# Branch weights prepared early and kept in DRAM, Fourier parts and share loads moved, projections reordered

## The chip, the cores and the metric

The kernel runs on one core of one Trainium2 chip. The metric is the device time of one execution in microseconds (us), taken as the median of several runs. The core has five engines: TensorE (PE, matmuls; its weight loads are listed as PEld), VectorE (DVE), ScalarE (ACT), GpSimd (POOL) and SyncE (SP). In this kernel SP issues most loads, and POOL issues stores, broadcasts, gathers and accumulating transfers. Each of the two works through its transfers in the order of the program and waits in front of one whose data or buffer is not ready.

## The reference

One encoder layer on a sequence of 1024 positions with 1024 channels, in float32. The middle step, in which the change lies, is the mixer:

```python
h = x @ w_in + b_in                       # -> q, k, v (12 heads of 128), u (4 groups of 128), gates
for g, (window, dilation) in enumerate(((128, 1), (512, 4), (2048, 16))):
    o, l = dilated_window_attention(q[:, :, sl], k[:, :, sl], v[:, :, sl], rel_bias[:, sl], window, dilation)
    outs.append(o); lses.append(l)
w_mix = softmax(stack(lses), axis=0)      # shares of the three groups
attn = sum(w_mix[..., None] * stack(outs), axis=0)
four = real(fft2(u, axes=(positions, channels of the group), norm='ortho'))
merged = g_attn * (attn @ w_proj_attn) + g_four * (four @ w_proj_fourier)
return merged @ w_out
```

Before the mixer and after it stands a SwiGLU feed-forward network; each of the three steps ends in a residual sum and a layer normalization.

## The kernel before

**Numbers.** A float32 product is made of three matmuls. `split` writes a page of 128x1024 as a high part (ScalarE, a copy rounded to fp32r) and a low part (VectorE, the difference), and high x high, high x low and low x high are summed. Most products are paired in a scheme with seven half-size products instead of eight (`pair_jobs`, line 443); one such product is 12 matmuls of 128x128 by 128x512.

**Order.** Nothing runs in the order of the source. The class `Flow` (lines 72 to 257) is a planner that runs while the program is written out. PE's jobs have a fixed order. Every other step is a node with an engine, a planned cost, nodes that it depends on, and for many the job that needs it and a lead. A load (`Q`) is written out when the plan's clock has come to within its lead of the job that needs it and enough pages are free; its landing is planned at `RATE` MB per us behind the loads before it, plus `LAND` = 2.5 us. Steps of VectorE (`V`) and ScalarE (`S`) are written out in the order in which the plan finds them ready and due. Floating PE steps (`F`) are put between jobs as soon as the plan finds them ready. So planned costs decide in which order each engine gets its instructions; on the chip each engine then keeps that order.

**Buffers.** SBUF holds 46 pages of 128x1024 floats (`page`) and 11 half pages (`half`); PSUM has eight banks. The plan counts them.

**The mixer in time.** First 24 value products (`VJ`, 24 matmuls each; v goes to DRAM by way of POOL's `v_spill` stores), then 22 paired projections: `u` (2, the Fourier channels), `q` (12 heads, each followed by its attention steps as floating work: scores `sc`, softmax, transposes `pt` into half pages `pT`, value products `pv`), and `s` (8, gates, which go to DRAM). The split parts of the layer's input take 28 pages until the last paired projection.

**Combine** (`combine`, line 1399). For each head the softmax statistics go to DRAM and come back rearranged by 12 small gathers (`comb_t`), VectorE makes the shares of the three groups, and POOL stores them (`comb`). For each half and group POOL then loads the shares, broadcast over the partitions, into a half page (`cb`, `load_c`, line 1447), SP loads the group's values (`pw`), VectorE multiplies and adds (`weigh`, `add`), and POOL stores the sum (`attn_d`, line 1467). Loads are written out as soon as the nodes ahead of them are, with their waits.

**Branch projections and output.** `PJ[c]` (attention, 24 matmuls) and `FJ[c]` (Fourier, 20 matmuls, three banks) for eight column blocks c; after each, VectorE multiplies with the gates, merges both branches (`gl`) and the merged block is split (`mg`). `WJ[0, m]` and `WJ[1, m]` are the output jobs over the blocks 0 to 3 and 4 to 7. The order is PJ0 to PJ4, PJ5 FJ0, PJ6 FJ1, PJ7 FJ2, FJ3, then WJ[0, 0] FJ4, WJ[0, 1] FJ5, WJ[0, 2] FJ6, WJ[0, 3] FJ7, and the rest of WJ. Two column blocks share a page of weights: `load` (line 1642 for attention, 1669 for Fourier) fetches it just ahead of its first job, the Fourier page is folded by two VectorE instructions (lines 1682, 1683) and both are split. The Fourier job needs the position transform, which runs as floating work between the attention jobs: `uc` pages loaded from DRAM (line 1488), channel products `fc`, their split into half pages, position products `fp`, and the middle row `mid` (lines 1593 to 1609).

Of the kernel before, what the change touches and what calls it, by code (L numbers as in the profile page):

```python
# [10 lines left out]
F32 = mybir.dt.float32  # L11
# [5 lines left out]
P = 128  # L17
# [27 lines left out]
class Node:  # L45


    def __init__(self, eng, cost, fn, deps=(), need=None, lead=0.0, tail=0.0, slack=4.0, banks=0, frees=0, pages=0,
                 gives=0, halves=0, hgives=0):
# [22 lines left out]
class Flow:  # L72

    RATE, LAND, KEEP = 0.22, 2.5, 6
# [209 lines left out]
def kernel(  # L284
# [1114 lines left out]
    def combine(h):  # L1399
# [39 lines left out]
        n = S(0.0, gathers, [(n, 4.0)], slack=20.0)  # L1439
        n = V(0.6, tops, [(n, 14.0)], slack=20.0)  # L1440
        n = S(0.25, lambda: nc.scalar.activation(T["e"], T["e"], AF.Exp), [n], slack=20.0)
        n = V(0.9, shares, [n], slack=20.0)
        for hf in range(2):
            cs = slice(hf * 512, (hf + 1) * 512)
            prev = None
            for g in range(3):
# [15 lines left out]
                qc = Q(PJ[0], 0.25, load_c, [(n, 4.0)] + wait, 400.0, halves=1)  # L1462
# [11 lines left out]
        q = Q(PJ[0], 0.5, load, [(T["n", 0], 5.0), (T["n", 1], 5.0)], 16.0, pages=1)  # L1474
# [8 lines left out]
    for gi in range(4):  # L1483
# [5 lines left out]
        q = Q(PJ[0], 0.5, load, [(uf_n[gi], 4.0)], 2.0 - gi, pages=1)  # L1489
        t_, s_ = divmod(gi, 2)  # L1490
        for i in range(2):
# [24 lines left out]
            n = S(0.42, hi, [f], halves=2 if s_ == 0 else 0, slack=2.0)  # L1516
# [41 lines left out]
    for t in range(2):  # L1558
# [25 lines left out]
        f = F(3.3, run, fold_n[t, 0] + fold_n[t, 1] + [pos_parts["n", 0], pos_parts["n", 1]], 3, hgives=4)  # L1584
# [16 lines left out]
    def mid_parts():  # L1601
        se = edge_terms(4, ms_["e"])
        mid = page("fmidT", F32R)
        nc.vector.tensor_copy(mid, zero.to_broadcast([P, 1024]))
        cosine_parts(ms_["p"][:4], se[:4], mid[0:4], mid[64:68])
        nc.vector.tensor_copy(mid[32:36, :CK], mid[0:4, :CK].bitcast(F32))
        four["mid"] = mid
    f = F(1.7, mid_run, fold_n[0, 0] + fold_n[1, 0] + [pos_parts["n", 0]], 2)
    four_n.append(V(3.0, mid_parts, [f] + four_n, frees=2, pages=1, slack=2.0))
    fl.later(four_n[-1], 0.0, gives=4)  # L1610

# [17 lines left out]
    gates, merged, PW = {}, {}, {}  # L1629
# [8 lines left out]
    for c in range(8):  # L1638
        c2, cc = divmod(c, 2)
        st = {}  # L1640
        if cc == 0:
            def load(c2=c2):
                PW["a", c2] = t = page(f"wpa{c2}")
                nc.sync.dma_start(as_k(t, 4), w_pa.rearrange("(k p) n -> p k n", p=P)[:, :, c2 * 256:(c2 + 1) * 256])
            split(f"wpa{c2}", lambda c2=c2: PW["a", c2], lambda p, c2=c2: PW.__setitem__(("a", c2), p),
                  [Q(PJ[c], 0.5, load, pages=1)], PJ[c])
# [18 lines left out]
    for c in range(8):  # L1665
        c2, cc = divmod(c, 2)
        st = {}
        if cc == 0:
            def load(c2=c2):
                PW["r", c2] = t = page(f"wpf{c2}")  # L1670
                cs = slice(c2 * 256, (c2 + 1) * 256)
                for s in range(2):
                    nc.sync.dma_start(t[64 * s:64 * s + 64, 0:512].rearrange("p (t n) -> p t n", t=2),
                                      w_pf.rearrange("(t s m) n -> s m t n", t=2, s=2)[s, 0:64, :, cs])
                nc.sync.dma_start(t[:, 512:1024].rearrange("p (t n) -> p t n", t=2),
                                  w_rev.rearrange("(t p) n -> p t n", p=P)[:, :, cs])

            def fold_w(c2=c2):

                raw = PW.pop(("r", c2))  # L1680
                PW["w", c2] = w = page(f"wfold{c2}")
                nc.vector.tensor_add(w[:, 0:512], raw[:, 0:512], raw[:, 512:1024])
                nc.vector.tensor_sub(w[:, 512:1024], raw[:, 0:512], raw[:, 512:1024])
# [199 lines left out]
```

## Time and profile before

| What | us |
|---|---|
| Three runs, median (lowest to highest) | 2125.58 (2124.34 to 2128.51) |
| The profiled execution | 2127.23 |
| Its span, first to last instruction | 2125.5 |
| VectorE busy in the span | 1352.0 |
| ScalarE busy in the span | 765.1 |
| POOL busy in the span | 226.5 |

The mean granted clock of TensorE over the span is 0.993 of its full rate, and the DMA engines moved 349.88 MB. The span is the profiled execution's, so a sum made from its rows stands against 2127.23 us, which is 1.65 us above the median of the runs. How to read it: TensorE is nearly always busy, so that the busy shares say little; the views that list what TensorE waited for, and the order of time around each of these places, say where the time that is not matmul lies.

### The profile page before, as it was taken

The numbers are of one execution on the slowest core, as the hardware profiler recorded it, in microseconds if no ns is written. First come the engines' busy times: TensorE is split into PE (matmuls) and PEld (weight loads), VectorE is DVE, ScalarE is ACT, GpSimd is POOL, SyncE is SP. The second block draws the span as 40 slices with busy tenths as digits, with TensorE's granted clock in tenths as the row PEclk, the third lists the DMA queues.
The fourth block names the chain that finished last, engine by engine and source line by source line (L and its number), as shares of the span: only waits on it lengthen the run. The fifth ranks groups of instructions, "written<-read, shape, count | busy, mean of one in ns | idle before, by whom it ended". The sixth has DMA issues, their size and how long they took to land.

```text
span 2125.5 us, 25406 instructions
## 1 busy us (share of the span) xinstructions
PE 2090.3 (98%) x9619; PEld 1736.9 (82%) x9619; DVE 1352.0 (64%) x1856; ACT 765.1 (36%) x1175; POOL 226.5 (11%) x395
## 2 busy tenths in 40 slices
PE   9999999999999999999899999899999999999998
PEld 7888888888888888888788888788788888888876
DVE  6766666674475278566566655867766666675476
ACT  4322222452353023444345333225422222244242
POOL 0121211000001100022132100000000101010000
PEclk9999999999999999999999999999999999999999
DMA  4357876596543217476765538232122223267832
GB/s 163 126 177 210 266 201 182 173 326 238 198 159 114 75 64 208 138 183 181 214 186 144 174 131 321 100 129 100 72 99 108 104 89 134 88 236 267 295 131 77
DMA packets 137050, 349.88 MB, mean 165 GB/s; under 512 B 17554, under 2 KB 39826, under 8 KB 136544
## 3 DMA queue, kind: packets, MB, share of 16 engines
q1 hardware_dynamic: 102304, 235.97, 31.9%
q0 software_dynamic: 34624, 112.30, 18.0%
q8 instruction: 75, 1.23, 0.2%
q14 instruction: 47, 0.39, 0.1%
HBM read 268.79 MB, written 128.67 MB: 187 GB/s over the span
## 4 chain that ended last, share of the span: by engine, by line
PE 91%; DVE 3%; issue 2%; DMA 2%; POOL 1%; ACT 1%; SPq 0%; DVEq 0%; POOLq 0%; ACTq 0%
PE Bb L421 7%; PE Ba L421 7%; PE v L1042 6%; PE Ab L421 5%; PE Db L421 5%; PE Da L421 4%; PE Aa L421 4%; PE Bq L421 4%; PE wo L1758 4%; PE Bs L421 3%; PE Xb L740 3%; PE Za L740 3%; PE Xa L740 3%; PE Zb L740 3%; PE Dq L421 2%
## 5 line engine op out<-in xcount | busy, mean ns | idle before, releaser
L1048 DVE TENSOR_TENSOR vs<-v,vb 128x512 f32<-128x512 f32 x24 | 16.5, 691 | 75.0 <-PE v L1042 70.2
L1292 ACT ACTIVATE p<-p,stat 128x192 f32<-128x192 f32 (+2 forms) x96 | 42.4, 445 | 33.5 <-DVE stat L1287 32.0
L1324 PE MATMUL pv<-pT,v 128*128 128x128 f32 (+1 forms) x320 | 42.2, 296 | 6.5 <-ACT pT L1313 6.5
L1324 PEld LDWEIGHTS pv<-pT,v 128*128 128x128 f32 (+1 forms) x320 | 38.5, 196 | 12.1 <-ACT pT L1313 6.9
L532 POOL DMA_DIRECT2D hsba<-r2b x19 | 10.3, 542 | 329.3 <-DVE r2b L602 329.3
L532 POOL DMA_DIRECT2D hsaa<-r2a x19 | 11.0, 580 | 281.4 <-DVE r2a L602 281.4
L1279 DVE SCALAR_TENSOR_TENSOR p<-sc,bias 128x512 f32<-128x512 f32 (+1 forms) x40 | 24.7, 620 | 23.9 <-PE sc L1265 20.4
L500 ACT ACTIVATE r1a<-Aa 128x512 f32<-128x512 f32 x19 | 11.4, 598 | 73.0 <-PE Aa L421 73.0
L508 DVE TENSOR_TENSOR r3b<-Bb,r1b 128x512 f32<-128x512 f32 x19 | 13.1, 692 | 36.4 <-PE Bb L421 36.4
L586 ACT ACTIVATE sga<-Aa 128x512 f32<-128x512 f32 x19 | 11.4, 599 | 64.3 <-PE Aa L421 64.3
L1265 PE MATMUL sc<-oq,oq 128*128 128x192 f32 (+2 forms) x192 | 34.0, 323 | 0.4 <-DVE oq L1086 0.4
L586 ACT ACTIVATE sgb<-Ab 128x512 f32<-128x512 f32 x19 | 11.4, 598 | 63.8 <-PE Ab L421 63.8
L589 DVE TENSOR_TENSOR r3b<-Db,r3b 128x512 f32<-128x512 f32 x19 | 13.1, 691 | 32.5 <-PE Db L421 32.4
L1265 PEld LDWEIGHTS sc<-oq,oq 128*128 128x128 f32 x192 | 29.8, 190 | 2.7 <-DVE oq L1086 0.8
L589 DVE TENSOR_TENSOR r3a<-Da,r3a 128x512 f32<-128x512 f32 x19 | 13.1, 691 | 29.3 <-PE Da L421 29.1
L1411 POOL DMA_DIRECT2D comb_t<-stat x48 | 29.2, 616 | 11.2 <-DMA stat<-stat 10.8
L1086 DVE SCALAR_TENSOR_TENSOR oq<-Dq,b_cols,r3q 128x512 f32<-128x512 f32 x12 | 11.8, 984 | 28.3 <-PE Dq L421 28.3
L500 ACT ACTIVATE r1b<-Ab 128x512 f32<-128x512 f32 x19 | 11.4, 599 | 47.6 <-PE Ab L421 47.6
L938 POOL DMA_DIRECT2D y_spill<-y x8 | 4.3, 537 | 215.4 <-DVE y L906 215.4
L492 DVE TENSOR_TENSOR usa<-ua,usa 128x512 fp32r<-128x512 f32 x19 | 13.2, 693 | 21.0 <-ACT usa L488 20.9
L421 PE MATMUL Db<-Zs40h,usb 128*128 128x512 f32 x76 | 26.5, 389 | 0.0
L421 PE MATMUL Db<-Zs41h,usb 128*128 128x512 f32 x76 | 26.5, 389 | 0.0
(7390 smaller groups left out, 7254.8 us busy)
## 6 DMA issues: line engine op xcount, KB each, us to landing
qa<-hsas SPq DMA_DIRECT2D x44, 256.0 KB, 4.6
qa<-tdat SPq DMA_DIRECT2D x44, 256.0 KB, 5.1
qb<-hsbs SPq DMA_DIRECT2D x44, 256.0 KB, 5.1
ga<-in_ffn_gu_dram SPq DMA_DIRECT2D x21, 512.0 KB, 4.1
ua<-in_ffn_gu_dram SPq DMA_DIRECT2D x21, 512.0 KB, 5.4
gb<-in_ffn_gu_dram SPq DMA_DIRECT2D x21, 512.0 KB, 3.5
ub<-in_ffn_gu_dram SPq DMA_DIRECT2D x21, 512.0 KB, 3.7
qa<-hsaa SPq DMA_DIRECT2D x33, 256.0 KB, 5.4
```

The source lines that it names most:

```text
L421: nc.tensor.matmul(out, pick(w, a)[:, k * P:(k + 1) * P], self.cols(xn, b, k), start=first and k == 0 and ti == 0, stop=last and k == 3 an ...
L500: nc.scalar.activation(H[c, "t1"], B[c, "A"], AF.Copy)
L586: nc.scalar.activation(H[c, "s0"], B.pop((c, "A")), AF.Silu)
L589: nc.vector.tensor_sub(H[c, "t3"], B[c, "D"], H[c, "t3"])
L740: nc.tensor.matmul(B[tag, set_, m], pick(q, a)[:, m * P:(m + 1) * P], pick(q, b)[:, R], start=first and j == 0 and ti == 0, stop=j == PAIR ...
L1042: nc.tensor.matmul(ps, X2.cols(f"a{hf + 1}{k // 4 + 1}", a, k % 4)[:, ms], pick(wv, b), start=(k == 0 and ti == 0), stop=(k == KD - 1 and ...
L1265: nc.tensor.matmul(sv[:, i, :], qk[0][:, qt * P:(qt + 1) * P], qk[1][:, k0:k0 + w], start=True, stop=True, skip_group_check=True)
L1279: stt(p3(), sv, scale, bv, op0=OP.mult, op1=OP.add)
L1292: nc.scalar.activation(p3()[:, i, :], p3()[:, i, :], AF.Exp, bias=stats[h][:, k, 0:1], scale=1.0, accum_out=stats[h][:, k, 1:2])
L1324: nc.tensor.matmul(out_of(tiles.index(qt)), env["v"][kc, rows], pt[r0:r0 + rows, sl * P:(sl + 1) * P], start=qt not in seen, stop=last, sk ...
L1411: nc.gpsimd.dma_start(dst, bass.AP(tensor=sd.tensor, offset=sd.offset + 48 * p0 + 2 * col, ap=ap))
L1758: nc.tensor.matmul(bk[i], pick(merged[k], a)[:, ms], pick(wo[k], b)[:, i * 512:(i + 1) * 512], start=(k == 4 * gi and ti == 0), stop=(k == ...
```

## The change

The transfer rate of the plan goes from 0.22 to 0.28 MB per us. Loads get an attribute `strict`: such a load is written out only when the plan's PE clock has reached the time at which the nodes ahead of it are done. The loads of shares get it, and their delay behind the shares goes from 4 to 8 us; the gathers are planned 1 us and the step behind them 2 us later.

The eight pages of branch weights are loaded, folded (the Fourier ones) and split ahead of the first paired projection, with a lead of 60 us, beside the value products; POOL stores both parts of each to DRAM, and later one load of two pages takes the place of load, fold and split. The page loads of the attention sums, of the Fourier parts and of the position matrices get longer leads, the Fourier products are split into pages instead of half pages, and the middle page is zeroed in a step of its own. The Fourier jobs move ahead in PE's order. The diff is cut to its core.

```diff
-    RATE, LAND, KEEP = 0.22, 2.5, 6
+    RATE, LAND, KEEP = 0.28, 2.5, 6
@@ issue
-            if n.left:
+            if n.left or (n.strict and n.time() > self.pe):
                 continue
@@ the order of the projections
-    branch_jobs(range(5), ())
-    for c in range(3):
-        branch_jobs((5 + c,), (c,))
-    branch_jobs((), (3,))
+    branch_jobs((0, 1, 2, 3, 4), (0,))
+    branch_jobs((5,), (1, 2))
+    branch_jobs((6,), (3,))
+    branch_jobs((7,), (4, 5))
     for gi in range(2):
         for m in range(8):
             WJ[gi, m] = job(24 * MM, None, 2, gives=16 if m == 7 else 0)
-            if gi == 0 and m < 4:
-                branch_jobs((), (4 + m,))
+            if gi == 0 and m < 2:
+                branch_jobs((), (6 + m,))
+    early = J[PC["u", 0], 1]
+
+    def keep_parts(name, load, deps, fold_=None):
+        st = {}
+        dst = [kb.dram([P, 1024], f"{name}_d{i}") for i in range(2)]
+        def run():
+            st["r"] = page(name)
+            load(st["r"])
+        q = Q(early, 0.5, run, deps, 60.0, pages=1)
+        if fold_:
+            def make():
+                raw = st["r"]
+                st["r"] = page(name + "s")
+                fold_(st["r"], raw)
+            q = V(1.38, make, [q], early, 52.0, 6.0, pages=1, gives=1)
+        def store():
+            for i in range(2):
+                nc.gpsimd.dma_start(dst[i], st["p"][i].bitcast(F32))
+        n = split(name + "e", lambda: st["r"], lambda p: st.__setitem__("p", p), [q], early, 52.0)
+        n = S(0.0, store, [n])
+        fl.later(n, 6.0, gives=2)
+        def again(key, need, lead):
+            def run():
+                PW[key] = t = page(name + "h", F32R), page(name + "l", F32R)
+                for i in range(2):
+                    nc.sync.dma_start(t[i].bitcast(F32), dst[i])
+            q = Q(need, 1.0, run, [(n, 6.0)], lead, pages=2)
+            need.after(q)
+        return again
...
+        kept["a", c2] = keep_parts(f"wpa{c2}", load_pa, [])
+        kept["f", c2] = keep_parts(f"wpf{c2}", load_pf, [(rev_n, 20.0)], fold_w)
@@ combine
-        n = S(0.0, gathers, [(n, 4.0)], slack=20.0)
-        n = V(0.6, tops, [(n, 14.0)], slack=20.0)
+        n = S(0.0, gathers, [(n, 5.0)], slack=20.0)
+        n = V(0.6, tops, [(n, 16.0)], slack=20.0)
-                qc = Q(PJ[0], 0.25, load_c, [(n, 4.0)] + wait, 400.0, halves=1)
+                qc = Q(PJ[0], 0.25, load_c, [(n, 8.0)] + wait, 400.0, halves=1, strict=True)
-        q = Q(PJ[0], 0.5, load, [(T["n", 0], 5.0), (T["n", 1], 5.0)], 16.0, pages=1)
+        q = Q(PJ[0], 0.5, load, [(T["n", 0], 5.0), (T["n", 1], 5.0)], 26.0, pages=1)
@@ Fourier parts
-        q = Q(PJ[0], 0.5, load, [(uf_n[gi], 4.0)], 2.0 - gi, pages=1)
+        q = Q(PJ[0], 0.5, load, [(uf_n[gi], 4.0)], 14.0 - gi, pages=1)
-                    fold[t_, i] = half(f"fh{t_}{i}", F32R), half(f"fl{t_}{i}", F32R)
+                    t = page(f"fold{t_}{i}", F32R)
+                    fold[t_, i] = t[:, 0:512], t[:, 512:1024]
-        q = Q(PJ[0], 0.5, load, (), 3.0, pages=1)
+        q = Q(PJ[0], 0.5, load, (), 22.0 - i, pages=1)
-                                  [q], PJ[3], 20.0)
+                                  [q], PJ[1], 26.0)
@@ the middle row
-        mid = page("fmidT", F32R)
-        nc.vector.tensor_copy(mid, zero.to_broadcast([P, 1024]))
+        mid = ms_["z"]
+    mz = V(0.7, mid_zero, [PJ[0]], pages=1, slack=2.0)
-    four_n.append(V(3.0, mid_parts, [f] + four_n, frees=2, pages=1, slack=2.0))
+    four_n.append(V(3.4, mid_parts, [f, mz, four_n[0]], frees=2, slack=2.0))
@@ projections: load, fold and split are gone
+            kept["a", c2](("a", c2), PJ[c], 28.0)
+            kept["f", c2](("f", c2), FJ[c], 24.0)
```

## Rows read from the trace of the kernel before

**Rows 1.** The page's first part: busy us by engine, share, instructions.

```profile
PE 2090.3 (98%) x9619; PEld 1736.9 (82%) x9619; DVE 1352.0 (64%) x1856; ACT 765.1 (36%) x1175; POOL 226.5 (11%) x395
```

**Rows 2.** What PE waited for: line, releaser: us in all, times, longest.

```profile
PE pv L1324 <- ACT pT L1313: 6.5, 1, 6.5
PE wo L1758 <- ACT mg2h L329: 4.1, 1, 4.1
```

**Rows 3.** PE in order of time: start, us, line, operation, [idle <-releaser].

```profile
1008.49 1.95 PE L1324 MATMUL pv<-pT,v 128*128 128x128 f32 x16
1010.27 0.93 PE L1308 MATMUL pt<-ident,p 128*128 128x128 f32 x7
1020.42 3.57 PE L1324 MATMUL pv<-pT,v 128*128 128x128 f32 x16 [6.46 <-ACT pT L1313]
1023.92 0.50 PE L421 MATMUL Bq<-Ya220h,t34q9h 128*128 128x512 f32 x1
```

**Rows 4.** Stretches: window, busy us by engine, granted clock, DMA share, GB/s.

```profile
1374.00:1376.00 2.00, 1.87 (x5) 0.95 (x3) 1.97 (x3) 0.00 (x0) 0.00 (x0) 0.50 0.00 0
```

**Rows 5.** Order of time on VectorE, POOL and ScalarE, around 1004 to 1020 us.

```profile
1003.58 0.68 DVE L1460 TENSOR_TENSOR pw<-pw,pw 128x512 f32<-128x512 f32 x1
1003.95 0.67 POOL L1437 DMA_DIRECT2D comb<-comb_e  x1 [8.23 <-DVE comb_e L1436]
1010.39 0.58 POOL L1450 DMA_DIRECT2D cb<-comb  x1 [5.77 <-DMA comb<-comb_e]
1010.96 0.55 POOL L1467 DMA_DIRECT2D attn_d<-pw  x1
1019.77 0.60 ACT L1313 ACTIVATE pT<-pt 128x512 f32<-128x512 f32 x1 [7.98 <-DMA attn_d<-pw]
```

**Rows 6.** PE in order of time, around the first two output jobs.

```profile
1365.98 0.62 PE L1758 MATMUL wo<-wo0h,mg0h 128*128 128x512 f32 x2
1377.86 1.22 PE L1758 MATMUL wo<-wo3h,mg3h 128*128 128x512 f32 x2 [1.99 <-ACT mg3h L329]
1384.36 0.61 PE L1758 MATMUL wo<-wo0h,mg0h 128*128 128x512 f32 x2
1389.80 0.28 PE L1697 MATMUL pfe<-fch,wfp2h 128*128 128x258 f32 x1
1392.86 0.61 PE L1758 MATMUL wo<-wo0h,mg0h 128*128 128x512 f32 x2
```

**Rows 7.** Stretches: before the first pair job; before the output projection.

```profile
738.00:779.00 41.00, 41.00 (x183) 33.95 (x182) 22.09 (x24) 7.22 (x7) 3.79 (x7) 1.00 0.21 74
1343.00:1376.00 33.00, 28.78 (x147) 23.97 (x145) 31.73 (x51) 11.39 (x13) 0.00 (x0) 0.94 0.39 128
```

**Rows 8.** VectorE's groups by line, 1343 to 1376 us: count, busy, mean ns.

```profile
L1682 DVE TENSOR_TENSOR wfold<-wpf 128x512 f32<-128x512 f32 x2 | 1.4, 686 | 0.0
L333 DVE TENSOR_TENSOR wfp1l<-wfold,wfp1h 128x1024 fp32r<-128x1024 f32 x1 | 1.2, 1219 | 0.0
```

**Rows 9.** VectorE in order of time, and the chain of work, first pair job.

```profile
780.83 1.22 DVE L333 TENSOR_TENSOR t34u0l<-t34u,t34u0h 128x1024 fp32r<-128x1024 f32 x1
...
787.21 2.72 PE Bu L421 x12
```

**Rows 10.** Stretches: around the first projection.

```profile
1290.00:1300.00 10.00, 10.00 (x46) 8.27 (x45) 6.24 (x7) 7.65 (x9) 1.11 (x2) 1.00 1.03 401
```

**Rows 11.** The tile `uc`: its instructions with first and last start, its landings.

```profile
L1495 PE MATMUL fc<-chan,uc x64: 270/275/275, 1311.1 to 1323.6; 128*128 128x128 f32 x64
L1488 SPq DMA_DIRECT2D uc<-uf_d x4: 377/391/775, 1285.5 to 1288.2; - x4
DMA to landing us min/median/max: 10.6/12.0/13.3
```

**Rows 12.** DMA issues by kind: count, KB each, median us from issue to landing.

```profile
v_spill<-vs POOLq DMA_DIRECT2D x24, 256.0 KB, 2.3
...
gq<-in_in_pairs_dram SPq DMA_DIRECT2D x12, 512.0 KB, 6.6
```

More of the change, by code (lines that the diff above doesn't have):

```diff
@@ L48, in __init__ @@
     def __init__(self, eng, cost, fn, deps=(), need=None, lead=0.0, tail=0.0, slack=4.0, banks=0, frees=0, pages=0,
-                 gives=0, halves=0, hgives=0):
+                 gives=0, halves=0, hgives=0, strict=False):
+        self.strict = strict
         self.eng, self.cost, self.fn, self.need, self.lead, self.tail, self.slack = eng, cost, fn, need, lead, tail, slack
@@ new lines, with load_pa, load_pf, fold_w @@
+    PW, kept = {}, {}
+    for c2 in range(4):
+        cs = slice(c2 * 256, (c2 + 1) * 256)
+        def load_pa(t, cs=cs):
+            nc.sync.dma_start(as_k(t, 4), w_pa.rearrange("(k p) n -> p k n", p=P)[:, :, cs])
+        def load_pf(t, cs=cs):
+            for s in range(2):
+                nc.sync.dma_start(t[64 * s:64 * s + 64, 0:512].rearrange("p (t n) -> p t n", t=2),
+                                  w_pf.rearrange("(t s m) n -> s m t n", t=2, s=2)[s, 0:64, :, cs])
+            nc.sync.dma_start(t[:, 512:1024].rearrange("p (t n) -> p t n", t=2),
+                              w_rev.rearrange("(t p) n -> p t n", p=P)[:, :, cs])
+        def fold_w(w, raw):
+            nc.vector.tensor_add(w[:, 0:512], raw[:, 0:512], raw[:, 512:1024])
+            nc.vector.tensor_sub(w[:, 512:1024], raw[:, 0:512], raw[:, 512:1024])
+        kept["a", c2] = keep_parts(f"wpa{c2}", load_pa, [])
+        kept["f", c2] = keep_parts(f"wpf{c2}", load_pf, [(rev_n, 20.0)], fold_w)
@@ L1515 @@
             f = F(0.88, run, [q, (chan_ready, 10.0)], 1, gives=i)
-            n = S(0.42, hi, [f], halves=2 if s_ == 0 else 0, slack=2.0)
+            n = S(0.42, hi, [f], pages=1 if s_ == 0 else 0, slack=2.0)
             fold_n.setdefault((t_, i), []).append(V(0.65, lo, [n], frees=1, slack=2.0))
@@ L1583, in sine_lo @@
             four[t] = (st["c"], (sp[:, 0:512], sp[:, 512:1024]))
-        f = F(3.3, run, fold_n[t, 0] + fold_n[t, 1] + [pos_parts["n", 0], pos_parts["n", 1]], 3, hgives=4)
+        f = F(3.3, run, fold_n[t, 0] + fold_n[t, 1] + [pos_parts["n", 0], pos_parts["n", 1]], 3, gives=2)
         n1 = V(0.3, edges, [f], frees=1, slack=2.0)
@@ L1607, in mid_parts, with mid_zero @@
         four["mid"] = mid
+    def mid_zero():
+        ms_["z"] = t = page("fmidT", F32R)
+        nc.vector.tensor_copy(t, zero.to_broadcast([P, 1024]))
     f = F(1.7, mid_run, fold_n[0, 0] + fold_n[1, 0] + [pos_parts["n", 0]], 2)
-    four_n.append(V(3.0, mid_parts, [f] + four_n, frees=2, pages=1, slack=2.0))
-    fl.later(four_n[-1], 0.0, gives=4)
+    mz = V(0.7, mid_zero, [PJ[0]], pages=1, slack=2.0)
+    four_n.append(V(3.4, mid_parts, [f, mz, four_n[0]], frees=2, slack=2.0))
+    S(0.0, lambda: None, list(four_n), gives=4)
     def mid_raw():
@@ L1641 @@
         if cc == 0:
[L1642 to L1646, printed above, removed]
+            kept["a", c2](("a", c2), PJ[c], 28.0)
         def run(c=c, c2=c2, cc=cc, st=st):
@@ L1668 @@
         if cc == 0:
[L1669 to L1683, printed above, removed]
-            q = Q(FJ[c], 0.5, load, [(rev_n, 20.0)], pages=1)
-            n = V(1.38, fold_w, [q], FJ[c], 16.0, 4.0, pages=1, gives=1)
-            split(f"wfp{c2}", lambda c2=c2: PW["w", c2], lambda p, c2=c2: PW.__setitem__(("f", c2), p), [n], FJ[c])
+            kept["f", c2](("f", c2), FJ[c], 24.0)
         def run(c=c, c2=c2, cc=cc, st=st):
```

2 lines of the change are left out of this document (1 added, 1 removed).

## The prediction

> **What bounds the kernel now.** I read the page's first part before anything else: TensorE (PE) is busy in 2090.3 us of a span of 2125.5 [rows 1]. So the kernel is a row of matmuls with holes, and a change that removes no matmul can win back at most the 35 us of holes, plus what the clock gives away after them. The second view is the list of what PE waited for [rows 2]: its largest entry is 6.5 us before one group of `pv` products (probabilities times values), and the next that lie in the code of this change are 4.1 and 2.0 us in the output projection (`wo`) [rows 2, 6]. The other holes (the first loads, the last normalization) are not touched by it. I then opened the two places in the order of time.
>
> Hole A, in the attention. One group of 16 `pv` matmuls starts at 1020.42 after 6.46 us without PE, and its next neighbour starts 3.50 us later; the group before took 1.78 us from its start to the start of the next [rows 3]. The reader is to see that a hole costs twice: idle time, then matmuls at the lower of the clock's two levels (1.2 instead of 2.4 GHz, granted clock 0.50; the row after hole B shows it [rows 4]). A costs 6.46 + (3.50 - 1.78) = 8.2 us.
>
> Its cause is a queue, not an engine [rows 5]. The tile `pT` needed a half page that the store `attn_d` of the combine was still reading. The sum to be stored was ready on VectorE (DVE) at 1003.58 + 0.68 = 1004.26, but the store left POOL's queue only at 1010.96: ahead of it stood a load of shares (`cb`) that waited 5.77 us for the store `comb` to land. The store then landed just before 1019.77.
>
> Hole B, between the branch projections and the output projection. The first output job starts at 1365.98 and the second at 1384.36 [rows 6]. Without a hole one output job takes 1389.80 - 1384.36 = 5.44 us and one Fourier job 1392.86 - 1389.80 = 3.06, so 8.50 us of work took 18.38: B costs 9.9 us, 6.1 of it idle [rows 2, 6] and the rest the lower clock. What PE waits for is the split of `mg2` and `mg3`, and in front of them VectorE is busy for 31.73 of 33 us [rows 7]: in this stretch VectorE is the bound.
>
> So A and B are worth 18.1 us together, 0.85% of the span. That is the most that this change can win by its own logic.
>
> **The change, part by part.**
>
> Weights made ready early. Each of four column blocks of the two branch weights was split (and the Fourier one folded) just ahead of its use. One fold is two VectorE instructions of 0.69, one split 1.22 on VectorE [rows 8]; its other half is on ScalarE, which has time. Of these, two folds and two splits lie in the 33 us before hole B: 4 x 0.69 + 2 x 1.22 = 5.2 us go from the chain that ends in `mg3`; the zeroing of the `mid` page moves ahead too. The same work, 8 x 1.22 + 4 x 2 x 0.69 = 15.3 us of VectorE, is put in front of the first projection after the value products. There VectorE is busy in 22.1 of 41 us [rows 7], so 18.9 us are idle: it fits, with 3.6 us to spare. If it does not fit there in time, the weights of the first pair job come late. Their slack: the split `t34u0l` ends at 782.05, and the product that reads it starts at 787.21 [rows 9], so 5.2 us can be lost before PE sees anything. I cost this part at nothing and keep 0 to 10 us as its bounds (15.3 us pushed whole behind 779, less 5.2 of slack).
>
> New transfers. Eight loads of 0.5 MB, sixteen stores of 0.5 MB on POOL's queue, and later 1.0 MB instead of 0.5 MB for each block on SP's queue. Among the value products the DMA engines are at a share of 0.21 [rows 7], so the first 12 MB are hidden. POOL's stores stand between the `v_spill` stores, and each waits for its split on VectorE; behind it stand only the next `v_spill`, whose half page no value product needs at once. No wait of these is on PE's path. Around the first projection it is otherwise: the share is 1.03 at 401 GB/s [rows 10]. Three blocks' reloads add 1.5 MB there, 1.5 / 0.401 = 3.7 us later landing for what is queued behind. The Fourier parts `uc` are issued up to 1288.2 and land within 13.3 us, by 1301.5; the matmuls on them start at 1311.1 [rows 11]: 9.6 us of slack, so this costs nothing, even before they are asked for 12 us sooner.
>
> What could make the stores late is how POOL issues them. In this stretch POOL's 24 `v_spill` stores land in 2.3 us in the median [rows 12], beside a VectorE that is busy more than half of the time: nothing holds them up. A rule of the Trainium skill speaks against the change here: "SBUF — State Buffer", "SBUF: two separate sides", says that a transfer issued from POOL has its descriptors written by POOL itself, which is shut out of a port that it shares with VectorE while some of VectorE's fp32 copies run. By the row the sixteen stores cost nothing and the sum stays. By the rule they would land late and hold their pages, and the time would be that of rival 2 below, 2120; I give it no more than a part of that rival's chance.
>
> Projections reordered. Fourier job 0 moves ahead of attention job 5, and jobs 4 and 5 move from behind the output jobs to ahead of them. Between Fourier job 3 and the first output job there now stand one attention job (as long as an output job, 24 matmuls of the same size, 5.44) and two Fourier jobs (6.1): 11.6 us more for the chain of `mg3`. Against this, jobs 4 and 5 bring VectorE their first step as well, and each takes three banks of eight. With 5.2 us gone from the chain alone, PE's products on `mg3` would start at 1377.86 - 5.2 = 1372.7 [rows 6] where they are wanted, by the old order, at 1365.98 + 0.75 x 5.44 = 1370.1: 2.6 us late. With the new order it is early. What is late next is VectorE's release of banks and pages: the output weights need 12 pages while the projections hold most of the 46. I give B a remainder of 0 to 4 us and take 1.5.
>
> Share loads later. Before, a load of shares entered POOL's queue as soon as the combine was written out, with its wait in front of whatever came next; now it enters 8 us (in the plan) after the shares are known, so the store of hole A would leave behind `comb` at about 1004.7 instead of 1010.96, 6.3 us sooner. If it lands as slowly as before (1019.77 - 1010.96 = 8.8 us), it lands at 1013.5, and `pT` ends at 1014.2 where PE became free at 1020.42 - 6.46 = 1013.96: 0.3 us of wait, and hardly a fall of the clock. The price is a later combine; only the last head's could reach PE, and it ends far ahead of the first projection. A goes down to 0.3, with a bound of 3. The longer planned delays work the same way.
>
> The planner's transfer rate, 0.22 to 0.28 MB/us. It moves every load's planned landing in the whole program, by 0.5/0.22 - 0.5/0.28 = 0.5 us for a half-MB load, so that splits can be placed ahead of loads that have not landed. No row shows what that does. Bounds: -2 us (the small holes shrink) to +8 us (one hole of A's size); I take +2, nearer the low end, because PE has no hole among the 22 pair jobs but A.
>
> Sum: A 8.2 - 0.3 = 7.9 and B 9.9 - 1.5 = 8.4 won, 2 lost: 14.3 us. The profiled execution took 2127.2 us (span 2125.5 and 1.7 around it), which gives 2112.9; it lies 1.6 above the median of the runs, 2125.6, so the time forecast is 2111.
>
> **The rivals.**
>
> 1. Only one hole closes. A stays if another store of the combine comes to stand behind a waiting POOL entry: the same queue still carries value stores and weight sums. Time: 2125.6 - 8.4 + 2 = 2119. B stays in half if pages or banks run out in front of the output projection: 2125.6 - 7.9 - 5 + 2 = 2115. For it: the SP queue there already waits for pages. Against it: 5.2 us less on VectorE is certain.
>
> 2. The cover of the early weights is gone. If pages come free only when the second third of the value weights is given back, near 738, the 15.3 us meet VectorE's own 22.1 in 41 us, and a few us of lateness put a stall on the first pair jobs: 10 us and 2 of lower clock at most. Time: 2111 + 8 to 12, about 2120. Against: 3.6 us to spare and 5.2 of slack.
>
> 3. Slower. The rate of 0.28 is faster than what the attention stage gets: a pair's load takes 6.6 us to land there in the median [rows 12], while the plan allows 0.5/0.28 + 2.5 = 4.3 (it allowed 4.8). VectorE and ScalarE run in the order planned, so a split placed too early holds up the scores' and values' steps behind it, and PE with them. The price is a hole like A, 8.2 us each; two eat the gain, and from three on (14.3 + 2 - 3 x 8.2 = -8.3) the kernel is slower: about 2134. For: the rate was raised for all stages, while only two had a hole. Against: only 0.5 us per load, against slacks like the 5.2 us above.
>
> 4. It does not do what it says: the loads asked for sooner wait for pages anyway, and the order is set by the same things as before. Then B keeps 6 us and A closes: 2116, inside case 1.
>
> **How the numbers follow.** The forecast, both holes nearly closed (2104 to 2115): 0.46. One closes, or B in half, with case 4 (2115 to 2120): 0.25. Case 2 (2117 to 2125): 0.10. Case 3: 0.15, of which 0.13 lies beyond 2130. Something unseen near no change: 0.04. About 0.2%, 4.3 us, is what a measurement of this kernel tells from no change. Faster, below 2121.3: 0.46 + 0.25 + half of case 2 = 0.76. Slower, above 2129.8: 0.13. The rest, 0.11, is the same. The range runs from 2103 (all 18.1 us and the small holes) to 2127, which leaves out case 3 and little else.
>
> **What would show it.** Right: PE's list of waits has no entry of `pv` above 1 us and none of `mg` above 2 us; the granted clock shows no slice under 0.95 in the attention and none between the projections; `attn_d` stores follow `comb` within 1 us; VectorE in the 33 us before the output projection has idle time; the folds stand between 720 and 780 us. Wrong: a new entry of PE on a `u` or `q` split (cases 2, 3), POOL entries that wait for landings ahead of stores, or a Fourier job that waits for banks. If the two holes are gone and the time is the same, the rate is to be asked first.

## The result and the profile after

| Kernel | Median us (lowest to highest, runs) | Ratio to before, 95% interval |
|---|---|---|
| before | 2127.91 (2124.34 to 2128.69, 5) | 1 |
| changed | 2102.89 (2102.25 to 2103.66, 5) | 0.9892 [0.9881, 0.9902] |

The changed kernel is 25.0 us faster by the medians (by the ratio 23.0, 20.9 to 25.3); 2111 was forecast, with a range from 2103 to 2127. So the direction was right, the time lies at the low end of the range (0.1 us below it), and the gain by the medians is 10.7 us larger than the sum of 14.3. The profiled execution of the changed kernel took 2102.25 us with a span of 2100.5; the spans too differ by 25.0.

The first part of the page after, busy us by engine, answers to [rows 1]:

```profile
PE 2081.6 (99%) x9619; PEld 1732.6 (82%) x9619; DVE 1353.3 (64%) x1856; ACT 766.6 (36%) x1175; POOL 234.9 (11%) x411
```

PE is idle in 2100.5 - 2081.6 = 18.9 us, where it was idle in 2125.5 - 2090.3 = 35.2. So 16.3 of the 25.0 us are holes that are gone, and 8.7 are matmul time: PE is busy in 8.7 us less with the same matmuls. Of these, 7.0 lie behind the three holes named below (1.7 behind A, 3.8 behind B, 1.5 behind C), where the granted clock was at 0.50 before. Another 1.3 us lie in the attention behind A at a granted clock of 1.00, and no run says why. The mean granted clock of the span went from 0.993 to 0.998.

What PE waited for, after (line, releaser: us in all, times, longest), answers to [rows 2]:

```profile
PE ga L422 <- ACT ga0h L330: 2.5, 1, 2.5
PE tpZ L373 <- DVE y L907: 1.7, 1, 1.7
PE warm L1832 <- DVE eps L310: 1.4, 1, 1.4
```

There is no entry of `pv` or of `wo`; the three largest that are left are the first loads, the last normalization and the start.

Where the 25 us went is read from the starts of three matmuls that stand at the ends of stretches: the first gate product (end of the attention), the first output product on the second half (end of the projections), and a late product of the last feed-forward network. In both kernels the same number of matmuls stands ahead of each (5211, 6603 and 9427), so that a difference of starts is a difference of time for the same work. PE in order of time, before:

```profile
1137.90 0.39 PE L421 MATMUL As<-Ya110h,gs14h 128*128 128x512 f32 x1
1431.62 0.61 PE L1758 MATMUL wo<-wo4h,mg4h 128*128 128x512 f32 x2
2068.84 0.80 PE L740 MATMUL Vb<-qb75l,qb75h 128*128 128x512 f32 x1 [2.69 <-DVE qb75l L333]
2072.78 0.39 PE L740 MATMUL Vb<-qb76h 128*128 128x512 f32 x1
```

The same view after:

```profile
1126.80 0.39 PE L422 MATMUL As<-Ya110h,gs14h 128*128 128x512 f32 x1
1410.70 0.62 PE L1798 MATMUL wo<-wo4h,mg4h 128*128 128x512 f32 x2
2045.03 0.39 PE L741 MATMUL Vb<-qb75l,qb75h 128*128 128x512 f32 x1
2047.52 0.39 PE L741 MATMUL Vb<-qb76h 128*128 128x512 f32 x1
```

The attention gave 1137.90 - 1126.80 = 11.1 us, the projections 1431.62 - 1410.70 - 11.1 = 9.8, and the stretch up to the last line 2072.78 - 2047.52 - 20.9 = 4.3. This last one is a third hole, C: 2.69 us idle before `qb75l`, and the lower clock behind it. It stood in the same list of waits as A and B, and the prediction passed over it.

Hole A, POOL and ScalarE in order of time after, answers to [rows 5]:

```profile
1005.86 0.66 POOL L1493 DMA_DIRECT2D comb<-comb_e  x1 [14.06 <-DVE comb_e L1492]
1007.20 0.58 POOL L1523 DMA_DIRECT2D attn_d<-pw  x1 [0.67 <-DVE pw L1516]
1013.35 0.54 POOL L1361 DMA_DIRECT2D pv_d<-pv  x1 [5.57 <-ACT pv L1338]
1013.88 0.55 POOL L1506 DMA_DIRECT2D cb<-comb  x1
1008.11 0.98 ACT L1314 ACTIVATE pT<-pt 128x384 f32<-128x384 f32 x2 [0.44 <-PE pt L1309]
```

The load of shares `cb` stands behind the store `attn_d`, and waits for nothing itself; `pT` waits for its own transposes (0.44) and for no transfer.

Two stretches of 33 and 41 us (busy us by engine, granted clock, DMA share, GB/s), the one before the output projection, which now starts at 1361.06, and the one ahead of the first pair job, answer to [rows 7]:

```profile
1328.00:1361.00 33.00, 33.00 (x180) 28.70 (x180) 27.62 (x46) 11.03 (x13) 0.00 (x0) 1.00 0.37 141
738.00:779.00 41.00, 41.00 (x182) 33.95 (x182) 32.99 (x37) 12.90 (x13) 10.18 (x19) 1.00 0.88 328
```

VectorE, which had 1.3 us idle in the first, has 5.4; in the second it is busy for 32.99 us, PE has no idle time, and the folds run from 731.4 to 762.2 (first and last instruction):

```profile
L1447 DVE TENSOR_TENSOR wpf0s<-wpf x1: 684/684/684, 731.4 to 731.4; 128x512 f32<-128x512 f32 x1
L1448 DVE TENSOR_TENSOR wpf3s<-wpf x1: 683/683/683, 761.5 to 761.5; 128x512 f32<-128x512 f32 x1
```

(VectorE's group by line: count, duration in ns, first and last start.)

### The profile page after: what moved, and what is told of

Same layout as the page of the kernel before. It is cut to its first block, busy times and chain, and to the rows that moved or that the text cites. A ratio compares the mean times of both kernels' runs of the same rounds, so it can differ in the third digit from the quotient of the medians.

```text
span 2100.5 us, 25488 instructions
## 1 busy us (share of the span) xinstructions
PE 2081.6 (99%) x9619; PEld 1732.6 (82%) x9619; DVE 1353.3 (64%) x1856; ACT 766.6 (36%) x1175; POOL 234.9 (11%) x411
## 4 chain that ended last, share of the span: by engine, by line
PE 86%; issue 2%; DVE 1%; ACT 0%; DMA 0%; POOL 0%; DVEq 0%; POOLq 0%; ACTq 0%
PE Bb L422 7%; PE v L1043 6%; PE Ab L422 5%; PE Db L422 5%; PE Bq L422 5%; PE Ba L422 4%; PE Dq L422 3%; PE Aq L422 3%; PE Bs L422 3%; PE Zb L741 3%; PE Xb L741 3%; PE Za L741 3%; PE Xa L741 3%; PE Da L422 2%; PE wo L1798 2%; PE Aa L422 2%
## 5 line engine op out<-in xcount | busy, mean ns | idle before, releaser
L533 POOL DMA_DIRECT2D hsba<-r2b x19 | 10.3, 543 | 329.8 <-DVE r2b L603 329.8
L501 ACT ACTIVATE r1a<-Aa 128x512 f32<-128x512 f32 x19 | 11.3, 597 | 73.0 <-PE Aa L422 73.0
L509 DVE TENSOR_TENSOR r3q<-Bq,r1q 128x512 f32<-128x512 f32 x12 | 8.3, 691 | 42.8 <-PE Bq L422 42.8
L493 DVE TENSOR_TENSOR usa<-ua,usa 128x512 fp32r<-128x512 f32 x19 | 13.1, 692 | 21.0 <-ACT usa L489 20.9
L422 PE MATMUL Da<-Xs40h,usa 128*128 128x512 f32 x76 | 26.5, 389 | 0.0
L422 PE MATMUL Da<-Xs41h,usa 128*128 128x512 f32 x76 | 26.5, 389 | 0.0
```

The costliest lines, as they stand in the source:

```text
L422: nc.tensor.matmul(out, pick(w, a)[:, k * P:(k + 1) * P], self.cols(xn, b, k), start=first and k == 0 and ti == 0, stop=last and k == 3 an ...
L501: nc.scalar.activation(H[c, "t1"], B[c, "A"], AF.Copy)
```

## The experiments

Five parts of the change were set apart: the rate, the later share loads, the early weights, the order, and the longer leads of the Fourier parts. Not set apart were the Fourier products in pages instead of half pages, the step that zeroes the middle page, and the longer lead of the attention sums: they are in every kernel made from the changed one, and in none made from the kernel before. Four kernels are the kernel before with one part alone, five the changed kernel with one part left out, two the kernel before with several parts, and one goes further with the rate. The kernel before was run again beside each group of them; its median there was 2126.71, 2123.52 and 2125.20 us, and the ratios stand against these. A gain or loss against the kernel before is worked out from the ratio; the difference of medians is up to 0.9 us off it. What it costs to leave a part out is the difference of medians to 2102.89, beside that of the spans; the changed kernel was not run again beside these groups, and the medians of the kernel before differ by up to 4.4 us between them.

### One part alone

**The rate.** The kernel before with

```diff
-    RATE, LAND, KEEP = 0.22, 2.5, 6
+    RATE, LAND, KEEP = 0.28, 2.5, 6
```

> The kernel before with the planner's rate raised from 0.22 to 0.28 and nothing else. Theory 1 (each part closes its own hole, and the rate closes the holes that lie far from the other edits): the hole before the last Strassen sums of the second feed-forward network (2.7 us idle and 1.4 of lower clock) and the small holes of the attention go, hole A (8.2) and hole B (9.9) stay: about 2122. Rival (the rate alone is the change: planned landings were too late everywhere, the other edits ride along): A and B shrink by half or more, 2113 or less. Rival (the rate is what costs): a new hole on a pair's split, 2130 or more.

Measured: 2123.71 us, ratio 0.9983 [0.9974, 0.9992], a gain of 3.6 us. The profiled execution was the slowest of its eleven (2127.3), so its holes may be larger than in most. What PE waited for:

```profile
PE sc L1265 <- DVE oq L1086: 7.1, 3, 3.4
PE wo L1758 <- ACT mg2h L329: 4.2, 1, 4.2
PE wo L1758 <- ACT mg3h L329: 2.3, 1, 2.3
```

Holes A and C are gone, with no other edit, and three new ones stand in the attention: scores that wait for `oq`. VectorE in order of time ahead of the longest:

```profile
1082.22 0.69 DVE L1457 TENSOR_TENSOR pw<-pw,cb 128x512 f32<-128x512 f32 x1 [5.22 <-DMA cb<-comb]
1083.96 0.74 DVE L1086 SCALAR_TENSOR_TENSOR oq<-Dq,b_cols,r2q 128x512 f32<-128x512 f32 x1
```

It is hole A's mechanism on another queue: the multiplication of the combine waits 5.22 us on VectorE for its shares, and the sums that PE needs stand behind it. VectorE's group of these multiplications had 5.0 us of such waits in all before, and has 18.2 now:

```profile
L1457 DVE TENSOR_TENSOR pw<-pw,cb 128x512 f32<-128x512 f32 x24 | 16.5, 688 | 18.2 <-DMA cb<-comb 18.2
```

By the three starts this execution wins C (4.3 us) and loses the rest again: the attention ends 2.2 us later than before although A's 8.2 are gone, and the projections lose another 2.2. So the rate is no small cost, as the prediction had it, but gains (A and C) and losses (mostly these holes) of about the same size. The sum of the waits for shares is not their price: in the changed kernel VectorE waits 8.4 us for them, and in that without the later share loads 8.6, but only the second has waits of PE behind them.

**The share loads.** The kernel before with

```diff
-            if n.left:
+            if n.left or (n.strict and n.time() > self.pe):
-        n = S(0.0, gathers, [(n, 4.0)], slack=20.0)
-        n = V(0.6, tops, [(n, 14.0)], slack=20.0)
+        n = S(0.0, gathers, [(n, 5.0)], slack=20.0)
+        n = V(0.6, tops, [(n, 16.0)], slack=20.0)
-                qc = Q(PJ[0], 0.25, load_c, [(n, 4.0)] + wait, 400.0, halves=1)
+                qc = Q(PJ[0], 0.25, load_c, [(n, 8.0)] + wait, 400.0, halves=1, strict=True)
```

> The kernel before with the share loads alone: strict, 8 us behind the shares, gathers and tops planned 1 and 2 us later; rate 0.22. Theory 1 (hole A is a store standing in POOL's queue behind a load of shares that waits for its landing): A's 8.2 us go, B and the last hole stay: about 2119, and the stores attn_d follow comb within 1 us. Rival (A went because the rate moved the whole attention): A stays, 2127.

Measured: 2119.09 us, ratio 0.9960 [0.9946, 0.9973], a gain of 8.5 us. What PE waited for:

```profile
PE wo L1759 <- ACT mg2h L330: 4.1, 1, 4.1
PE Vb L741 <- DVE qb75l L334: 2.4, 1, 2.4
PE wo L1759 <- ACT mg3h L330: 2.3, 1, 2.3
PE Bs L422 <- DVE r3s L509: 1.5, 1, 1.5
```

A is gone, B and C stand as before. The store did not come sooner, though, as the expectation had it: `attn_d` leaves POOL at 1025.34, 13.8 us behind `comb`, after 7.07 us of waiting for its own sum. So leaving the share loads later takes A away, but not by the store close behind `comb`; why `pT` finds a half page in this plan was not traced. By the starts of the same matmuls as above, the product behind hole A came 7.8 us sooner than before and the end of the attention 10.2: A itself, and 2.4 us behind it. Of these one piece is seen in the trace of before: VectorE waits 1.79 us for `cb` at 1106.97, and PE 0.5 us for a split (`t12q13l`) behind it. New is the wait for `r3s` in the gate products, 1.5 us, so that not all of the 10.2 arrives.

**The early weights.** The kernel before with `keep_parts` and the reloads as shown in the diff, everything else as before.

> The kernel before with the branch weights folded, split and stored beside the value products, in the old order of projections and at the old rate. Theory 1 (hole B is VectorE's backlog, 5.2 us of it folds and splits): B falls from 9.9 to about 3, A stays: 2120. Rival (B is a matter of order, the chain from the last Fourier job to the first output job): B stays above 7, 2125. Either way no new hole on the first pair job, if the 15.3 us of VectorE fit in the idle 18.9; a hole there would add up to 10.

Measured: 2131.03 us, ratio 1.0017 [1.0008, 1.0027], 3.6 us slower. What PE waited for:

```profile
PE fc L1549 <- DMA uc<-uf_d: 5.1, 1, 5.1
PE pv L1324 <- ACT pT L1313: 3.8, 1, 3.8
PE wo L1791 <- ACT mg3h L329: 2.7, 1, 2.7
PE wo L1791 <- ACT mg2h L329: 1.9, 1, 1.9
```

Of B's 6.1 idle us 4.6 stay, and of its price of 9.9 us 7.3 (the second output job starts 15.75 us after the first instead of 18.38): the rival's more than 7, not the theory's 3. No pair job waits. But the Fourier parts `uc` come too late, by a hole of 5.1 us that no other kernel here has; between the end of the attention and the first output job 8.1 us are lost. Their landings, of before in [rows 11]:

```profile
L1549 PE MATMUL fc<-chan,uc x64: 270/275/550, 1297.5 to 1321.6; 128*128 128x128 f32 x64
DMA to landing us min/median/max: 13.9/16.0/17.2
```

Both ends of the 9.6 us of slack moved. The landing takes 16.0 us in the median instead of 12.0, and the planner puts the first `fc` at 1297.5 instead of 1311.1. The DMA engines carry 407 GB/s from 1285 to 1318 where they carried 337, but while the `uc` loads are on their way they are full in both kernels (397 GB/s from 1285 to 1302 before, 407 from 1283 to 1304 here, at a share of 1.03), so this does not explain the later landing.

**The order.** The kernel before with the edit of `branch_jobs` as in the diff.

> The kernel before with the projections reordered alone. Theory 1 (VectorE is the bound, so 11.6 us more between Fourier job 3 and the first output job hide most of its backlog, but jobs 4 and 5 add their own first steps): B falls from 9.9 to 2 to 5, A stays: 2121 to 2123. Rival (the order alone closes B): 2118. Rival (banks: each Fourier job takes three of eight and VectorE releases them late): a new wait of PE before a Fourier job, 2127 or more.

Measured: 2127.99 us, ratio 1.0006 [0.9997, 1.0015]. What PE waited for:

```profile
PE pv L1324 <- ACT pT L1313: 6.8, 1, 6.8
PE pfe L1701 <- DVE fmidT L1606: 3.9, 1, 3.9
PE pfe L1697 <- DVE wfp3l L333: 2.0, 1, 2.0
PE pfe L1697 <- DVE fch L1547: 1.6, 1, 1.6
```

The waits for `mg2` and `mg3` are gone, so the order alone, without VectorE's 5.2 us, takes away B's old cause. In its place the Fourier jobs, which now come sooner, wait 7.5 us for their own chain (`fch`, `fmidT`) and for their weights (`wfp3l`). The hole has only moved. The time is that of the rival on banks, but not by its cause: what the Fourier jobs wait for is their inputs.

### One part left out of the changed kernel

**Without the rate** (0.22 in place of 0.28):

> The changed kernel with the rate put back to 0.22. Theory 1 (the rate closes only the holes far from the other edits): the hole before the last sums of the second feed-forward network comes back (about 4), and 1 to 3 us in the attention: 2107 to 2110; A and B stay closed. Rival (the rate is the change): A and B come back at least in half, 2114 or more.

Measured: 2112.44 us, ratio 0.9948 [0.9935, 0.9962]; leaving it out costs 9.6 us (10.2 of span). What PE waited for:

```profile
PE pfe L1741 <- DVE fmidT L1662: 3.2, 1, 3.2
PE Vb L741 <- DVE qb75l L334: 2.4, 1, 2.4
```

C is back, and so is the wait for the Fourier chain; A stays closed. By the three starts 0.8 us are lost up to the end of the attention, 6.6 in the projections and 2.7 at C. That lies between theory and rival: of the change's 9.8 us in the projections two thirds hang on the rate.

**Without the later share loads** (`gathers` 4.0, `tops` 14.0, `load_c` 4.0 and no `strict`):

> The changed kernel with the share loads as before (not strict, 4 us, gathers 4 and 14). Theory 1: a hole of A's kind comes back in the attention, 5 to 8 us: 2108 to 2111. Rival (A was closed by the rate or by the new order of everything): 2103.

Measured: 2109.66 us, ratio 0.9940 [0.9927, 0.9954]; costs 6.8 us (7.2 of span). No wait on `pT`, but as with the rate alone:

```profile
PE sc L1266 <- DVE oq L1087: 4.4, 2, 2.3
```

and in front of the first of them, VectorE in order of time:

```profile
1079.21 0.69 DVE L1513 TENSOR_TENSOR pw<-pw,cb 128x512 f32<-128x512 f32 x1 [4.09 <-DMA cb<-comb]
1080.95 0.74 DVE L1087 SCALAR_TENSOR_TENSOR oq<-Dq,b_cols,r2q 128x512 f32<-128x512 f32 x1
```

So with the rate in, the share loads are no longer there for hole A but for these.

**Without the early weights** (load, fold and split just ahead of use, as before):

> The changed kernel with the branch weights loaded, folded and split just ahead of their use, as before. Theory 1 (VectorE's 5.2 us matter, but the new order gives 11.6): B comes back by 1 to 4 us: 2104 to 2107. Rival (the early weights carry B's gain): 5 us or more, 2108 and above. Rival (order and earlier Fourier parts carry all of it): 2103.

Measured: 2105.09 us, ratio 0.9913 [0.9898, 0.9929]; costs 2.2 us (2.3 of span), by one wait of a Fourier job for `wfp3l` of 1.9 us. A difference of medians as small as this would not be safe alone, but the starts agree: 2.3 us are lost in the projections, where the wait stands.

**Without the new order** (the four `branch_jobs` lines of before):

> The changed kernel with the old order of the projections. Theory 1 (with VectorE relieved by 5.2 us the chain to the first output job is 2.6 us late by the old order, plus some lower clock): 2105 to 2107. Rival (the order carries B's gain): 8 us or more, 2111. Rival (the order does nothing once the weights are early): 2103.

Measured: 2112.13 us, ratio 0.9940 [0.9927, 0.9954]; costs 9.2 us (8.9 of span). With all other parts in, B comes back at 7.4 of its 9.9 us (the second output job starts 15.94 us after the first):

```profile
PE wo L1798 <- ACT mg3h L330: 2.7, 1, 2.7
PE wo L1798 <- ACT mg2h L330: 1.9, 1, 1.9
```

The products on `mg3` in order of time:

```profile
1365.90 1.22 PE L1798 MATMUL wo<-wo3h,mg3h 128*128 128x512 f32 x2 [2.66 <-ACT mg3h L330]
```

**Without the longer Fourier leads:**

```diff
-        q = Q(PJ[0], 0.5, load, [(uf_n[gi], 4.0)], 14.0 - gi, pages=1)
+        q = Q(PJ[0], 0.5, load, [(uf_n[gi], 4.0)], 2.0 - gi, pages=1)
-        q = Q(PJ[0], 0.5, load, (), 22.0 - i, pages=1)
+        q = Q(PJ[0], 0.5, load, (), 3.0, pages=1)
-                                  [q], PJ[1], 26.0)
+                                  [q], PJ[3], 20.0)
```

> The changed kernel with the loads of the Fourier parts and the splits of the position spectra due as late as before; all else as changed. Theory (these due times are needed under the new order): PE waits for fmidT, fch or posp in the first Fourier jobs, 2 to 6 us idle and the lower clock after it, 2106 to 2111. Rival (with the weights made early and the rate of 0.28 there is room enough): no such wait above 1 us, 2102 to 2104.

Measured: 2109.54 us, ratio 0.9925 [0.9912, 0.9938]; costs 6.7 us (6.6 of span), by the expected waits. The first product on the middle row, PE in order of time, and the step of VectorE that it waits for:

```profile
1332.77 0.41 PE L1741 MATMUL pfe<-fmidT,wm 128*128 128x258 f32 x1 [3.16 <-DVE fmidT L1662]
1332.20 0.42 DVE L1662 CAST fmidT<-fmidT 4x514 fp32r<-4x514 f32 x1
```

The same two in the changed kernel:

```profile
1327.81 0.28 PE L1741 MATMUL pfe<-fmidT,wm 128*128 128x258 f32 x1
1326.17 0.42 DVE L1662 CAST fmidT<-fmidT 4x514 fp32r<-4x514 f32 x1
```

With the leads the chain ends 1.2 us ahead of its product; without them PE waits for it. No `fc` waits for `uc` here: the loads land in 15.8 us in the median, the last by 1295.9, and the first `fc` starts at 1305.9.

### Several parts, and a further step

**Order and Fourier leads**, at the old rate: the order of the diff and the three lines above, the other way round. (The zeroed middle page, which the expectation names, stayed as before.)

> The kernel before with the new order of the projections and the Fourier parts (position spectra, folded parts, the zeroed middle page) loaded and made sooner; weights as before, share loads as before, rate 0.22. Theory (the order moves the hole to the Fourier chain and the sooner parts close it; early weights are not needed): PE waits neither for mg2/mg3 nor for fmidT or fch, hole A (pv on pT, 6 to 7 us) and the hole on qb75l (2.4 to 2.7 us) stay; about 9.8 us less than before, 2117 (2114 to 2119). Rival (VectorE's 5.2 us of folds and splits are what matters, so that without the early weights a hole of 3 us or more stays in front of wfp3 or fmid): 2121 or more.

Measured: 2120.81 us, ratio 0.9975 [0.9965, 0.9986], a gain of 5.3 us, which lies between the two theories. The first waits of PE's list but for the first loads:

```profile
PE pv L1324 <- ACT pT L1313: 6.6, 1, 6.6
PE Vb L740 <- DVE qb75l L333: 2.4, 1, 2.4
PE pfe L1697 <- DVE wfp3l L333: 1.9, 1, 1.9
```

No wait for `mg`, `fch` or `fmidT` is left, so order and leads together do take B away; but the wait for `wfp3l`, which the theory had at nothing, keeps a part of the price (5.6 of the 9.8 us in the projections are won), and it is the wait that the early weights take away.

**Order, Fourier leads and rate:**

> The kernel before with the new order, the Fourier parts sooner and the rate of 0.28: the change without the early weights and without the later share loads. Theory (parts are worth what leaving each out of the changed kernel cost: early weights 2.2 us, share loads 6.8 us, and they don't meet): 2103 + 2.2 + 6.8 = 2112 (2109 to 2114), no PE wait on mg, fmidT, fch or qb75l above 1.9 us, and two or three waits of the scores for oq of 2 to 3.5 us each. Rival (the early weights keep the share loads or the queue short, so that both left out cost more than their sum): 2116 or more, with a hole on pT.

Measured: 2113.86 us, ratio 0.9946 [0.9932, 0.9960], at the upper end of 2109 to 2114. PE waits for `oq` (4.0 us, twice), for `wfp3l` (1.9) and for `r3s` (1.5): the prices of the two parts that are missing nearly add up (2.2 + 6.8 = 9.0 against 11.0), and no hole on `pT` opens. The edits that were not set apart are missing too, so at most about 2 us are left for them, if the prices add.

**A rate of 0.34** in the changed kernel:

> The changed kernel with the planner's rate at 0.34 instead of 0.28 (a half-MB load is planned to land in 1.5 + 2.5 us instead of 1.8 + 2.5). Theory (the rate's gain is that splits are no longer planned behind loads that have long landed, and most of it is had at 0.28): no new entry among PE's waits, 2100 to 2104. Rival (0.28 is a matched setting; a plan that is more hopeful than the landings puts splits in front of data that is not there): new waits of scores or values for q, k or v tiles, 2107 or more.

Measured: 2103.11 us, ratio 0.9894 [0.9880, 0.9909]; the span is 0.2 us longer, and the list of waits has no new entry. The gain of the rate is had at 0.28, and nothing is lost at 0.34. None of the kernels beats the changed one.

## Why the prediction was right, and where it was not

**What bounds the kernel, and the 18.1 us.** Reading the list of waits of PE and opening each place was right, and so was counting a hole twice: behind A, B and C 7.0 of the 25.0 us are clock. The step that failed is "that is the most that this change can win by its own logic", with the other holes "not touched". The list had a third hole of the same size as B's parts, `Vb` on `qb75l`, and one term of the change, the rate, moves every step of the plan. Before, the split of `qb75` stood on VectorE behind the last normalizations of a block, and ran at 2067.56; in the changed kernel it runs at 2018.90, ahead of them. VectorE in order of time, before and after:

```profile
2067.56 1.22 DVE L333 TENSOR_TENSOR qb75l<-qb,qb75h 128x1024 fp32r<-128x1024 f32 x1
2018.90 1.23 DVE L334 TENSOR_TENSOR qb75l<-qb,qb75h 128x1024 fp32r<-128x1024 f32 x1 [4.21 <-ACT qb75h L330]
```

The rate alone does it (2044.2 there, and no wait of PE), and without the rate the hole is back.

**Hole A.** Won 7.9 forecast. The product behind it starts 1029.50 - 1020.78 = 8.7 us sooner (0.5 of which was there before the attention), so 8.2: right in price. In the changed kernel the queue does what was worked out: `attn_d` follows `comb` by 1.34 us (the sign named was 1), of which 0.67 is the wait for its own sum, and not by 7.01 as before. The 1004.7 for `attn_d` was 2.5 us too soon, as `comb` itself left POOL 1.9 us later than before; a landing of 5.6 us instead of 8.8 made up for it. That the late store made the hole is read from the trace of before; it is not the only way out of it. The same store leaves 13.8 us behind `comb` with the share loads alone and 8.7 us ahead of it (1000.47) with the rate alone, and A is gone in both. So A belonged to one arrangement of the plan, and either edit breaks it. Not in the sum were 2.4 us behind A in the attention: 1.1 of them idle time, of which 0.5 stand behind a wait for `cb`, the rest matmul time.

**Hole B.** Won 8.4 forecast, 9.8 measured: the remainder of 1.5 did not come. Size and place were right, but the carrier was mis-sized. The prediction took all of VectorE's 5.2 us off the chain that ends in `mg3`, and so left 2.6 to the order. Without the new order the products on `mg3` start at 1365.90, where a job without a hole that starts at 1356.25 has them at 1356.25 + 0.75 x 5.44 = 1360.3: 5.6 us late, and as late with the early weights alone. Before it was 1377.86 - 1370.1 = 7.8, so 2.2 of the 5.2 us arrived. VectorE is busy there for 27.5 us of 33 (1333.3 to 1366.3), where it was for 31.73: more than half of its relief became idle time in front of products of PE and copies of ScalarE. That PE's last wait, 2.7, is near the 2.6 worked out is chance: it stands behind a wait of 1.9 for `mg2`.

In the changed kernel the early weights are worth 2.2 us, the order 9.2, the Fourier leads 6.7 and the rate 9.6 (2.7 of it C). The four can't be added: of the 9.8 us in the projections 7.4 are lost without the order, 6.6 without the rate and 6.2 without the leads, so that each of these brings back most of B, but only 2.3 without the weights. What was not asked of the order was what it makes late: PE's need for the Fourier chain moves ahead, and the chain with it only by the leads, which the text costed at nothing.

**The early weights' own cost.** To cost them at nothing was right: the 22.1 + 15.3 = 37.4 of 41 us that were worked out bound the 32.99 measured (a part of the work ran ahead of 738, from 730.2 on), and no pair job waits. The DMA share there, 0.88, is far from the 0.21 of before, so "hidden" holds with less to spare than the text said: the sixteen stores took 4.0 to 11.3 us to land, and the `v_spill` stores among them 3.3 to 8.9, where the median had been 2.3. No instruction waited for them, and rival 2 did not come. What the rule of the Trainium skill ("SBUF — State Buffer", "SBUF: two separate sides") would make of the stores can't be told from this: they are late beside a DMA share of 0.97 (731 to 766 us), and no run here parts the two.

**`uc`.** "9.6 us of slack, so this costs nothing" failed where the weights stood alone: PE waits 5.1 us. The later landing was sized about rightly, 3.7 us worked out and 4.0 measured in the median. What failed is the other end: the slack had been measured to the place of `fc` in the old plan, and a floating step has no fixed place. In the changed kernel `uc` is issued by 1275.5 and lands in 10.3 us in the median, and the first `fc` at 1294.6 waits for nothing. The longer leads are not what saves it, as without them `fc` does not wait either; the hole belongs to the one plan.

**The rate.** +2 us was taken from bounds of -2 to +8. Alone it gained 3.6 [1.7 to 5.5], and in the changed kernel it is worth 9.6: outside of the low bound, which counted small holes only. The high end was not idle, though: new holes in the attention, rival 3's price, are what the rate alone shows (7.1 us idle in three holes), if by late shares on VectorE and not by splits. The later share loads take these away. So the sum of 14.3 missed 0.3 in A, 1.4 in B, 2.4 behind A, 4.3 in C, 2 for a rate that costs nothing, which makes 24.7, and 0.5 that was gained ahead of the attention: there the profiled executions of these kernels lie between 0.6 us sooner and 0.8 later than before, so it can't be put down to the change.

**Left open.** How the rate brings the Fourier chain ahead when the longer leads are in already was not traced through the plan; the runs only show that without it `fmidT` is 3.2 us late, and that the first `fc` starts at 1301.4 instead of 1294.6 although `uc` has landed by 1289.9. Nor were the two edits of the share loads, the delays and `strict`, run apart from each other.

## What to carry to other kernels

Where each engine keeps a planned order, look in the trace for any instruction that waits long for a transfer, on every queue, and read what stands behind it: here late loads of shares cost 8.2 us on POOL's queue in one plan and 6.8 us on VectorE's in another. A parameter that moves every planned time is to be priced against the whole list of waits, not against the places that the change is about. And a reordering has two sides: list what it makes early, then what it makes needed sooner, since the parts that look like trimmings (12 us more lead) can be what the gain hangs on.

## What was not expected of the hardware

The kernel with the holes varies more from run to run: the runs of the kernel before lie between 2120.63 and 2129.84 us, those of the changed kernel, five only, between 2102.25 and 2103.66.

A wait of the same length does not always bring the lower clock. PE waits 2.39 us for `qb75l` in the kernel with the early weights alone and in the changed kernel without the rate. Behind it the granted clock is 0.50 in the first (2071.5 to 2073) and 1.00 in the second (2055 to 2057), and hole C costs 4.2 us in the first and 2.7 in the second. So the second part of a hole's price has to be read behind the hole.

With the DMA engines at a share of 0.97 (731 to 766 us), the half-MB stores of the weights landed late, and so did the six quarter-MB stores `v_spill` that the same engine issued among them (3.3 to 8.9 us). The slowest of the sixteen (KB, us to landing), and the landings of all 24 `v_spill` stores (line 1050) of the changed kernel:

```profile
wpa_d<-wpa2el POOLq DMA_DIRECT2D x1, 512.0 KB, 11.3
DMA to landing us min/median/max: 2.3/2.8/8.9
```
